# The end of the first layer's experts: where the retention weights are split, when a tile's expert sum is added, and when two modulation chunks are computed

## The chip, the cores and the metric

One core of one Trainium2 chip runs the whole kernel. The metric is the device time of one execution in microseconds (us). Five engines work side by side, each through its own instruction queue: TensorE (PE, with its weight loads as PEld), VectorE (DVE), ScalarE (ACT), GpSimd (POOL) and SyncE (SP), which here issues most of the loads. Dependencies between engines are semaphores.

## The reference, cut to what matters

The network has two layers over 256 latent tokens and 256 context tokens of width 1024, in fp32. Layer 0 is a Fourier and neighbourhood-attention mixer and a mixture of 16 experts; layer 1 is retention with four heads and another mixture. What concerns this change is the seam between them:

```
f  = moe_ffn(tok, ...)                     # tok: 256 context rows, then 256 latent rows
hc = hc + g2c * f[:n_c]                    # layer 0's end, context
h  = h  + g2  * f[n_c:]                    # layer 0's end, latent
xm = modulate(rmsnorm(h,  g), sh1, sc1)    # layer 1's beginning
cm = modulate(rmsnorm(hc, g), sh1c, sc1c)
q, k, v, g = split(xm @ w_in)              # retention, latent
_, kc, vc, _ = split(cm @ w_in)            # retention, context (keys and values are used)
```

The modulation vectors are `silu(c) @ ada_w[layer] + ada_b[layer]`, six of width 1024 for each layer.

## The kernel before, in words

**Numbers.** Every fp32 product of weight and activation is made as three fp32r matmuls: each operand is split in a high half (ScalarE rounds it, `whi`, L176) and a low half (the difference, `wlo`, L178). `weight` loads a 1 MB tile of [128, 2048] by one DMA on SP's queue (`load`, L157) and splits it in two pieces of [128, 1024]. Its `pool` argument says how many of the two low halves GpSimd computes instead of VectorE. The raw tiles lie in a ring of slots, four of them at the end of the experts; a load waits until the slot's former tile has been read by all its users. The halves lie in a second ring, six slots there.

**Tokens.** The tokens are four tiles of 128 rows in `h`: tiles 0 and 1 are latent, 2 and 3 are context. The experts run one after the other; experts 0 to 14 add their rows into a DRAM sum `F` by an indirect DMA of GpSimd. `add_sum(t)` (L798 to L802) loads tile t of that sum into one of two buffers (`facc[:, t % 2]`), multiplies it by the gate row and adds it to `h`. Expert 15 does not scatter: its output stays on the chip as `yh`, `yl` (L1085, L1086), and `combine(t)` brings it to tile t's rows by a one-hot matmul (L792, L793), a multiplication from PSUM (L782) and an addition (L783), for two halves of the width.

**The seam.** `moe0_tail` normalises the context tiles first: `norm_scale` squares a tile on ScalarE (L322), runs a chain of one-column Newton steps for the inverse root on VectorE (L199 to L210, L324, L325) and scales the tile (L327). `norm_mod` transposes it on TensorE (L338), modulates it (L343, L346) and splits it into `r_xc` (L348, L349). Then come the v projection of the first context tile (`vproj`) and the key projection of both (`k_ctx`) for head 0. `retention` goes on with the second context tile's v projection, the same norms for the latent tiles, and then the latent v projections.

**Modulation chunks.** Each chunk of 512 columns of `ada_w` is two raw tiles and 64 small matmuls (L274), whose sum stands in a PSUM buffer until its finish adds the bias (L282) and writes the row to DRAM. Chunks 4 and 5 of layer 1 are the gate `g1`, which is first used behind the retention heads. `ada_step` does the next chunk of `ada_q`.

**Order.** A planner orders each engine's instructions by when they are ready in its model, and by the order in which they are written where several are. `issue_after(i)` adds an edge: what the block writes on the engine of `i` comes after `i` on that engine; other engines' instructions in the block get no edge. On the chip each engine runs its list in order.

Of the kernel before, what the change touches and what calls it, by code (L numbers as in the profile page):

```python
# [110 lines left out]
class Net:  # L111
# [609 lines left out]
    def moe0_tail(self, ep, psp, hps):  # L721
        nc, X = self.nc, self.X
        xr = self.pool(self.ret_es, "r_ctx", 1, side="right")
        self.xc = [xr.tile([128, 8, 256], F32R, name=f"r_xc{i}") for i in range(2)]
        self.kc = [xr.tile([128, 2, 256], F32R, name=f"r_kc{i}") for i in range(2)]
        self.v0 = xr.tile([128, 512], F32, name="r_v0")
        self.ret_wv = wv = [self.weight(("ret_w_in", (), 4 * i, 4, 2048, 512), 2) for i in range(2)]
        self.ret_w0 = w0 = self.weight(self.ret_keys(0)[0], 2)
        self.ada_q = [(1, c) for c in (4, 5, 6, 7, 8, 9)]
        hp = hps, "h"  # L730
        after = lambda i: self.tc.issue_after(i.ins)
        x = X["xg"]
        xms = lambda: ep.tile([128, 4, 128], F32, tag="g", name="xm")
        mm, add = self.combine(2)
        last = self.norm_scale(2, x[0])
        with after(last):
            mm, add = self.combine(3)
        last = self.norm_scale(3, x[1])
        with after(last), after(mm):
            self.ada_step(hp, psp)  # L740
        for t in (0, 1):
            self.add_sum(t)
        for t in (2, 3):
            last = self.norm_mod(1, t, x[t - 2], xms, psp, *self.xc)
        with after(last):
            for t in (0, 1):
                self.combine(t)
        v = hps.tile([128, 512], F32, tag="h", name="v_ps")
        self.vproj(wv, self.xc, 0, v)
        nc.scalar.copy(self.v0, v)  # L750
        self.k_ctx(w0, hps.tile([128, 2, 256], F32, tag="h", name="k_ps"), slice(0, 256))
        self.ada_step(hp, psp)

    def vproj(self, ws, x, t, ps):
        tk = slice(128 * t, 128 * t + 128)
# [293 lines left out]
    def expert(self, e):  # L1049
        nc, X = self.nc, self.X  # L1050
        layer, NT, ep, psp, hs, R, T = (X[k] for k in ("layer", "NT", "ep", "psp", "hs", "R", "T"))
        gw = R["gw"][:, e:e + 1]
        self.e_hid(e, "moe_w1", 1)
        self.e_hid(e, "moe_w3", 0)
        self.e_tr(e + 1)
        self.e_gather(e + 1 + len(X["xg"]))
        self.e_hid(e, "moe_w3", 1)
        g = ep.tile([128, 512], F32, tag="g", name="g")
        nc.scalar.activation(g, hs[e, "moe_w1"], AF.Silu)
        nc.vector.tensor_tensor(g, g, hs[e, "moe_w3"], ALU.mult)  # L1060
        gh = ep.tile([128, 4, 128], F32R, tag="gh", name="gh")
        gl = ep.tile([128, 4, 128], F32R, tag="gl", name="gl")
        self.transpose_split(g, 4, gh, gl, psp)
        self.e_hid(e + 1, "moe_w1", 0)
        if e < 15:
            y = ep.tile([128, D], F32, tag="y", name="y")
        else:
            S = ep.tile([128, T], F32R, name="S", bufs=1)
            self.onehot(S, NT, R["tokf"][:, e:e + 1])
            yh = ep.tile([128, D], F32R, name="yh", bufs=1)  # L1070
            yl = ep.tile([128, D], F32R, name="yl", bufs=1)
            X["y"] = S, yh, yl
            wts = [self.weight(("moe_w2", (layer, e), 0, 4, 512 * n, 512)) for n in range(2)]
            for t in (2, 3):
                self.add_sum(t)
        for n in range(2):
            ns = slice(512 * n, 512 * n + 512)
            wt = wts[n] if e == 15 else self.weight(("moe_w2", (layer, e), 0, 4, 512 * n, 512))
            ps = X["yps"].tile([128, 512], F32, tag="y", name="y_ps")
            for k in range(4):  # L1080
                self.mm3(ps, (gh[:, k], gl[:, k]), self.wk(wt, k), k == 0, k == 3)
            if e < 15:
                nc.scalar.activation(y[:, ns], ps, AF.Copy, scale=gw)  # L1083
            else:
                nc.scalar.activation(yh[:, ns], ps, AF.Copy, scale=gw)  # L1085
                nc.vector.scalar_tensor_tensor(yl[:, ns], ps, gw, yh[:, ns].bitcast(F32), ALU.mult, ALU.subtract)  # L1086
        if e < 15:
            nc.gpsimd.indirect_dma_start(out=self.F[:, :],  # L1088
                                         out_offset=bass.IndirectOffsetOnAxis(ap=R["tok"][:, e:e + 1], axis=0),
                                         in_=y, in_offset=None, bounds_check=T - 1, oob_is_err=False,  # L1090
                                         compute_op=ALU.add)
# [556 lines left out]
```

## Time and profile before

| | us |
|---|---|
| median of 3 runs (lowest 1306.22, highest 1993.7) | 1308.19 |
| the profiled execution | 1309.31 |
| its span, from the first to the last instruction | 1307.3 |

| engine | busy us | share of the span |
|---|---|---|
| PE | 1202.9 | 92% |
| PEld | 946.0 | 72% |
| DVE | 944.2 | 72% |
| ACT | 752.0 | 58% |
| POOL | 143.2 | 11% |

The shares are averages over the whole span; the seam is about 50 us of it, so it has to be read by stretch. In the profile's tables a row names line, engine, operation, output and inputs, the shape, how often, and in brackets how long the engine had been idle before it and which instruction ended that. Operations of the same line that follow each other are merged in a timeline (x2, x3). A matmul's end is modelled, and successive matmuls overlap.

### The profile page before, as it was taken

What the parts mean: (1) busy time and instruction counts of PE and PEld (TensorE: products, weight loads), DVE (VectorE), ACT (ScalarE), POOL (GpSimd) and SP (SyncE); (2) the same over time, 40 slices, a digit from 0 to 9 for tenths busy, and PEclk for the clock granted to TensorE, in tenths of its full rate; (3) what the DMA queues carried; (4) which work ended last, traced back from release to release, by engine and by line L of the source; (5) the groups of instructions that cost most, each with busy time, mean ns of one, the idle gap of its engine ahead of it and who ended that gap; (6) DMA issues with size and microseconds to landing.
All of it is one profiled execution on the core that took longest, in us unless ns stands there. A gap on an engine that the chain in (4) does not pass through costs nothing. (4 is left out here: it accounts for less than half of the span.)

```text
span 1307.3 us, 18799 instructions
## 1 busy us (share of the span) xinstructions
PE 1202.9 (92%) x7081; PEld 946.0 (72%) x7081; DVE 944.2 (72%) x1584; ACT 752.0 (58%) x1116; POOL 143.2 (11%) x138
## 2 busy tenths in 40 slices
PE   4999999897699999999589999999996999999994
PEld 3777666475588888777368888898775778877673
DVE  4755566866698988898876554554657889888985
ACT  3754565723488887877534333343434778767672
POOL 2010001201221112110500000000003100000010
PEclk8999999999799999999889999999998999999997
DMA  9766663444899999999745345432749899889980
GB/s 357 251 243 249 239 217 124 150 146 144 328 366 383 372 361 358 359 361 363 276 162 200 133 159 202 158 114 97 284 169 380 326 342 379 329 328 352 329 325 9
DMA packets 61413, 340.60 MB, mean 261 GB/s; under 512 B 10300, under 2 KB 14908, under 8 KB 24704
## 3 DMA queue, kind: packets, MB, share of 16 engines
q1 hardware_dynamic: 47232, 307.26, 62.5%
q0 software_dynamic: 11344, 27.62, 6.7%
q10 hardware_dynamic: 2736, 4.41, 1.0%
q8 instruction: 59, 0.97, 0.3%
q14 instruction: 42, 0.34, 0.1%
HBM read 331.64 MB, written 18.40 MB: 268 GB/s over the span
## 5 line engine op out<-in xcount | busy, mean ns | idle before, releaser
L178 DVE TENSOR_TENSOR wlo<-raw,whi 128x1024 fp32r<-128x1024 f32 x465 | 551.1, 1219 | 115.6 <-ACT whi L176 113.6
L176 ACT ACTIVATE whi<-raw 128x1024 fp32r<-128x1024 f32 x476 | 480.0, 1053 | 101.1 <-PE qk_ps L314 22.1
L314 PE MATMUL h_ps<-wlo,xh 128*128 128x512 f32 x512 | 206.9, 404 | 5.5 <-DVE wlo L178 5.4
L313 PE MATMUL h_ps<-whi,xh 128*128 128x512 f32 x512 | 205.1, 401 | 1.2 <-ACT xh L669 1.2
L315 PE MATMUL h_ps<-whi,xl 128*128 128x512 f32 x512 | 204.3, 399 | 0.0
L314 PEld LDWEIGHTS h_ps<-wlo,xh 128*128 128x128 f32 x512 | 96.9, 189 | 38.6 <-DVE wlo L178 18.8
L313 PEld LDWEIGHTS h_ps<-whi,xh 128*128 128x128 f32 x512 | 97.2, 190 | 22.7 <-ACT xh L669 1.6
L315 PEld LDWEIGHTS h_ps<-whi,xl 128*128 128x128 f32 x512 | 97.0, 189 | 20.3 <-DVE xl L670 0.3
L274 PE MATMUL ada_ps<-raw,cT 128*32 128x128 f32 x1536 | 54.5, 280 | 1.1 <-DMA raw<-in_ada_w 1.1
L313 PE MATMUL y<-whi,gh 128*128 128x512 f32 x128 | 51.6, 403 | 0.7 <-ACT gh L669 0.7
L313 PE MATMUL y_ps<-whi,gh 128*128 128x512 f32 x128 | 51.2, 400 | 0.7 <-ACT gh L669 0.7
L315 PE MATMUL y<-whi,gl 128*128 128x512 f32 x128 | 50.8, 405 | 0.8 <-DVE gl L670 0.6
L314 PE MATMUL y<-wlo,gh 128*128 128x512 f32 x128 | 51.1, 399 | 0.3 <-DVE wlo L178 0.3
L314 PE MATMUL y_ps<-wlo,gh 128*128 128x512 f32 x128 | 51.1, 399 | 0.0
L274 PEld LDWEIGHTS ada_ps<-raw,cT 128*32 128x32 f32 x1536 | 42.1, 111 | 12.1 <-issue 8.6
L315 PE MATMUL y_ps<-whi,gl 128*128 128x512 f32 x128 | 50.3, 403 | 0.1
L1088 POOL DMA_INDIRECT moe_sum<-y,tok x15 | 27.9, 1857 | 153.8 <-ACT y L1083 153.8
L669 ACT ACTIVATE gh<-tsp 128x512 fp32r<-128x512 f32 x32 | 19.1, 596 | 43.4 <-PE tsp L666 43.2
L313 PE MATMUL qk_ps<-xhi,whi 128*128 128x512 f32 x96 | 39.4, 411 | 0.0
L314 PE MATMUL qk_ps<-xlo,whi 128*128 128x512 f32 x96 | 38.8, 404 | 0.0
L315 PE MATMUL qk_ps<-xhi,wlo 128*128 128x512 f32 x96 | 38.4, 400 | 0.0
L1541 POOL DMA_INDIRECT out_dram<-hg,tok x4 | 6.6, 1662 | 274.5 <-DVE hg L1535 219.5
(438 smaller groups left out, 2423.9 us busy)
## 6 DMA issues: line engine op xcount, KB each, us to landing
raw<-in_moe_w SPq DMA_DIRECT2D x192, 1024.0 KB, 7.9
raw<-in_ada_w SPq DMA_DIRECT2D x48, 1024.0 KB, 5.1
raw<-in_ret_w_in SPq DMA_DIRECT2D x24, 1024.0 KB, 4.9
raw<-in_mixab_w_in SPq DMA_DIRECT2D x10, 1024.0 KB, 6.8
raw<-in_ret_w_out SPq DMA_DIRECT2D x8, 1024.0 KB, 4.8
raw<-in_mixab_w_out SPq DMA_DIRECT2D x4, 1024.0 KB, 6.7
bias<-in_rpb ACTq DMA_DIRECT2D x12, 256.0 KB, 4.9
g<-mod POOLq DMA_DIRECT2D x6, 512.0 KB, 4.7
```

The source lines that it names most:

```text
L176: self.nc.scalar.activation(hi, r, AF.Copy)
L178: eng.tensor_tensor(lo, r, hi.bitcast(F32), ALU.subtract)
L274: mm = nc.tensor.matmul(ps[32 * j:32 * j + 32, 0:128], self.cT[:, kk, :], raw[:, k, 128 * j:128 * j + 128], start=(kk == 0), stop=(kk == 7 ...
L313: mm(out, lh, rh, start=first, stop=False)
L314: mm(out, lh, rl, start=False, stop=False)
L315: self.mm_last = mm(out, ll, rh, start=False, stop=last)
L669: nc.scalar.activation(hi[:, b0:b0 + w], tv, AF.Copy)
L1088: nc.gpsimd.indirect_dma_start(out=self.F[:, :], out_offset=bass.IndirectOffsetOnAxis(ap=R["tok"][:, e:e + 1], axis=0), in_=y, in_offset=N ...
L1541: self.nc.gpsimd.indirect_dma_start(out=self.out[:, :], out_offset=bass.IndirectOffsetOnAxis(ap=idx, axis=0), in_=x, in_offset=None, bound ...
```

## The change

The six low halves of the three retention weight tiles (two for v, one for the keys) were GpSimd's; they become VectorE's. The two tiles for v are written behind tile 3's scale, so their low halves follow it on VectorE; the tile for the keys is written behind the last of the modulated context rows. Tile 3's expert sum is added in the tail behind tile 2's norm and no longer within expert 15. Tile 3's combine loses its edge. Chunks 4 and 5 are loaded and multiplied ahead of tile 3's norm, with both finishes behind the modulated context rows; before, chunk 4 came after the second norm and chunk 5 at the end. The sums of tiles 0 and 1 move behind the modulated context rows too.

```diff
-        self.ret_wv = wv = [self.weight(("ret_w_in", (), 4 * i, 4, 2048, 512), 2) for i in range(2)]
-        self.ret_w0 = w0 = self.weight(self.ret_keys(0)[0], 2)
-        self.ada_q = [(1, c) for c in (4, 5, 6, 7, 8, 9)]
+        self.ada_q = [(1, c) for c in (6, 7, 8, 9)]
...
         mm, add = self.combine(2)
         last = self.norm_scale(2, x[0])
+        self.add_sum(3)
+        mm, add = self.combine(3)
+        fin = [self.ada_mm(1, c, hp, psp) for c in (4, 5)]
+        last = self.norm_scale(3, x[1])
         with after(last):
-            mm, add = self.combine(3)
-        last = self.norm_scale(3, x[1])
-        with after(last), after(mm):
-            self.ada_step(hp, psp)
-        for t in (0, 1):
-            self.add_sum(t)
+            self.ret_wv = wv = [self.weight(("ret_w_in", (), 4 * i, 4, 2048, 512)) for i in range(2)]
         for t in (2, 3):
             last = self.norm_mod(1, t, x[t - 2], xms, psp, *self.xc)
         with after(last):
+            self.ret_w0 = w0 = self.weight(self.ret_keys(0)[0])
+            for f in fin:
+                f()
             for t in (0, 1):
+                self.add_sum(t)
                 self.combine(t)
...
         self.k_ctx(w0, hps.tile([128, 2, 256], F32, tag="h", name="k_ps"), slice(0, 256))
-        self.ada_step(hp, psp)
...
             wts = [self.weight(("moe_w2", (layer, e), 0, 4, 512 * n, 512)) for n in range(2)]
-            for t in (2, 3):
-                self.add_sum(t)
+            self.add_sum(2)
```

## Rows read from the trace of the kernel before

**Rows 1.** Stretches: length, busy PE PEld DVE ACT POOL, granted clock, DMA share, GB/s.
```profile
637.80:642.60 4.80, 2.64 (x9) 1.16 (x7) 3.82 (x6) 4.11 (x5) 4.02 (x2) 0.96 1.00 423
642.60:655.20 12.60, 0.12 (x1) 0.00 (x0) 11.50 (x15) 3.34 (x6) 10.80 (x5) 0.50 0.82 291
655.20:668.00 12.80, 7.96 (x81) 5.28 (x82) 11.27 (x27) 3.99 (x10) 0.26 (x1) 0.77 0.63 239
668.00:693.30 25.30, 25.15 (x249) 21.64 (x248) 16.22 (x48) 10.27 (x25) 1.59 (x3) 0.97 0.42 142
693.30:960.00 266.70, 265.66 (x1645) 228.15 (x1642) 145.65 (x229) 103.39 (x141) 6.44 (x12) 1.00 0.46 169
```

**Rows 2.** VectorE's timeline, 641 to 656 us: start, duration, instruction, [idle before].
```profile
641.06 1.29 DVE L782 TENSOR_TENSOR gtmp<-f_ps,g 128x512 f32<-128x512 f32 x2 [0.27 <-PE f_ps L793]
642.26 4.32 DVE L783 TENSOR_TENSOR h<-h,gtmp 128x512 f32<-128x512 f32 x2
647.38 1.44 DVE L324 TENSOR_TENSOR rms_ss<-nss 128x1 f32<-128x1 f32 x1 [0.79 <-ACT xg L322]
...
649.42 1.70 DVE L206 SCALAR_TENSOR_TENSOR rs_a<-rs_y,rs_h 128x1 f32<-128x1 f32 x1
651.15 2.26 DVE L210 SCALAR_TENSOR_TENSOR rs_y<-rs_a,rs_y 128x1 f32<-128x1 f32 x1
...
654.34 0.75 DVE L327 TENSOR_SCALAR xg<-h,rs_y 128x1024 f32<-128x1024 f32 x1
```

**Rows 3.** GpSimd's timeline, 638 to 656 us.
```profile
638.58 14.82 POOL L178 TENSOR_TENSOR wlo<-raw,whi 128x1024 fp32r<-128x1024 f32 x6 [15.22 <-ACT whi L176]
```

**Rows 4.** VectorE's timeline, 660 to 683 us.
```profile
660.02 1.22 DVE L801 TENSOR_TENSOR facc<-facc,g 128x1024 f32<-128x1024 f32 x1
...
666.48 0.75 DVE L327 TENSOR_SCALAR xg<-h,rs_y 128x1024 f32<-128x1024 f32 x1
...
676.23 1.28 DVE L783 TENSOR_TENSOR h<-h,gtmp 128x512 f32<-128x512 f32 x2
677.60 0.16 DVE L324 TENSOR_TENSOR rms_ss<-nss 128x1 f32<-128x1 f32 x1
...
678.36 0.22 DVE L206 SCALAR_TENSOR_TENSOR rs_a<-rs_y,rs_h 128x1 f32<-128x1 f32 x1
...
679.52 0.15 DVE L210 SCALAR_TENSOR_TENSOR rs_y<-rs_a,rs_y 128x1 f32<-128x1 f32 x1
682.12 0.69 DVE L768 SCALAR_TENSOR_TENSOR r_kc<-k_ps,r_kc 128x512 fp32r<-128x512 f32 x1 [2.45 <-ACT r_kc L767]
```

**Rows 5.** The low halves' line over the whole span: ns min/median/max.
```profile
L178 DVE TENSOR_TENSOR wlo<-raw,whi x465: 1192/1218/1277, 24.8 to 1286.3; 128x1024 fp32r<-128x1024 f32 x155
```

**Rows 6.** ScalarE's timeline, 637 to 641 us.
```profile
637.43 2.00 ACT L176 ACTIVATE whi<-raw 128x1024 fp32r<-128x1024 f32 x2 [1.05 <-DMA raw<-in_ret_w_in]
639.34 0.67 ACT L1085 ACTIVATE yh<-y_ps,gw 128x512 fp32r<-128x512 f32 x1
```

**Rows 7.** SP's queue (issue of loads), and raw tiles' landing times, 618 to 690 us.
```profile
629.44 2.17 SPq L157 DMA_DIRECT2D raw<-in_ret_w_in  x3
...
DMA to landing us min/median/max: 4.8/5.9/11.0
```

**Rows 8.** TensorE's timeline, 637 to 694 us.
```profile
637.59 0.39 PE L315 MATMUL y_ps<-whi,gl 128*128 128x512 f32 x1
655.62 1.94 PE L274 MATMUL ada_ps<-raw,cT 128*32 128x128 f32 x32
...
681.38 2.37 PE L274 MATMUL ada_ps<-raw,cT 128*32 128x128 f32 x74
...
683.88 0.48 PE L313 MATMUL v_ps<-whi,r_xc 128*128 128x512 f32 x1
...
689.56 0.82 PE L338 MATMUL nT<-cst,og 128*128 128x128 f32 x6
...
693.34 0.50 PE L313 MATMUL v_ps<-whi,r_xl 128*128 128x512 f32 x1
```

## The prediction

> **What bounds the kernel now.** I read the busy times by stretch first, then the VectorE, GpSimd, ScalarE, DMA-queue and TensorE timelines of one place: the end of layer 0's experts, 637 to 694 us.
>
> TensorE sets the pace after this place: from 693.3 to 960 us it is busy for 265.66 of 266.70 us at full granted clock [rows 1]. Before that it is not: it idles 12.5 of the 12.6 us from 642.6, and 4.8 of the next 12.8 [rows 1]. With 2.2 us just ahead (2.64 busy of 4.80) and 0.15 behind, that is 19.6 us of idle time, the most that this change can win. What is won here arrives at the end only because of that dense stretch: its 1% of idle time leaves nowhere for an earlier start to be absorbed. VectorE is nearly full in the same stretches (11.50 of 12.60, 11.27 of 12.80) but has 9.1 us free in the 25.3 us after them [rows 1].
>
> Why TensorE waits: the first transposes need tile 2's normalised rows, which VectorE finishes at 655.09, the last row of [rows 2]. Its chain there is slow. GpSimd runs six low halves of retention weights from 638.58 to 653.40 [rows 3]. Inside that span a pair of adds took 4.32 us, the one-column sum 1.44, the two Newton steps 1.70 and 2.26 [rows 2]; the same instructions later took 1.28, 0.16, 0.22 and 0.15 [rows 4]. The excess is 3.04 + 1.28 + 1.48 + 2.11 = 7.9 us. A product from PSUM, 1.29 us a pair, was not slowed [rows 2]. Nor is DMA traffic the cause: an SBUF-SBUF product at 660.02 took its usual 1.22 us [rows 4] while 239 GB/s moved [rows 1].
>
> The Trainium skill, "SBUF — State Buffer", section "Who interferes with whom", says that a VectorE instruction with two SBUF inputs and a GpSimd instruction that reads SBUF exclude each other for a whole instruction. By it the full 7.9 us go once GpSimd has no such work; were it wrong and the slow rows due to something else, this term would be 0 and the forecast would land where the second rival does. The unslowed PSUM product agrees with it.
>
> **Part by part.** Clock times are those of the trace.
>
> *GpSimd's six low halves go to VectorE.* Removed from the first chain: 7.9 us. Added: 6 x 1.22 = 7.3 us of VectorE [rows 5], but behind the second normalisation. GpSimd's later work is only small row writes, which nobody in this stretch waits for.
>
> *ScalarE.* The second half of yh ran at 639.34, behind two high halves that began at 637.43 [rows 6]. That half of y was ready when its matmuls ended, at 638.0 [rows 8]. With the ada loads taking the first slots, those high halves are not there yet: -1.3 us. Bound: 0, if the planner puts other splits there.
>
> *Tile 3's sum and combine.* Its two full-width instructions (2 x 1.2 = 2.4 us) ran before the second yl. They may now fall in the wait for y's second half (about 636.4 to 638.7, as long as they are): 0, or 2.4 us if that cover is gone and they enter the chain. The combine's VectorE half (four instructions, 2 x 1.28 = 2.5 us) is no longer held behind tile 2's scale, so it can enter tile 2's chain while ScalarE squares: +2.5 at worst, 0 at best; I take 2.4, since the old order kept tile 3's adds out by an explicit edge.
> Tile 2 is then ready at 655.1 - 1.3 - 7.9 + 2.4 = 648.3.
>
> *Tile 3's normalisation.* It ended at 667.23 because its one-column steps alternated with the sums of tiles 0 and 1, one of which is the 1.22 us row at 660.02 [rows 4]. These move behind the modulation. Alone, the chain is 2.1 us (677.60 to 679.67) plus 0.75 for the scale [rows 2, 4]: ready at 648.3 + 2.8 = 651.1, 16 us sooner.
>
> *Weights.* Four ada loads (1 MB each) now stand on SP's queue ahead of the three retention loads, with two small bias loads. The first load that was issued at 629.44 [rows 7] served a ScalarE split at 637.43 that had waited for it [rows 6]: 8.0 us. The ada halves take that place, are read by 32 matmuls each (1.94 us at the low clock), and free slots from about 639.5 and 641. With 8.0 us more the value weights land at 647.5 and 649, and with a high half of 1.05 us each (2.00 a pair [rows 6]) their last low half can begin at 651. VectorE is at 651.1 then: hidden, with about 3 us to spare behind the first halves. Landings in this stretch run from 4.8 to 11.0 us [rows 7]; 11.0 uses that spare up.
> VectorE then does four low halves (4.9) and tile 2's two lower halves of modulated rows (the key product's, of the same shape, took 0.69 [rows 4]): 657.3.
>
> *TensorE.* The v projection, 24 matmuls, takes 5.7 us (683.88 to 689.56 for the second one [rows 8]); it can start at about 656 and end by 662.7. Tile 3's modulation (two such halves, 1.4, and four pieces of 128x128, which hold the elements of one 0.69 us instruction: 0.7 to twice that, I take 1.3) and the key weights' two low halves (2.4) end at 662.4; the key projection, 48 matmuls of half the width, takes the same 5.7 us, which put its end at 681.38 [rows 8]: now 668.4. The second ada chunk, 64 of the 74 matmuls in 2.37 us (2.05 us), stood here [rows 8] and is now in the idle gap; so the next v projection, 5.7 us, ends at 674.1. The transposes and the filler chunk that took 3.8 us (689.56 to 693.34 [rows 8]) bring the latent v projection to 677.9, against 693.34: -15.4.
>
> *VectorE's floor for the same point.* From 662.4: two ada finishes (128x128 each; at most 0.69, I take 0.3 each), sums of tiles 0 and 1 (4 x 1.22), their combine (8 x 0.64, the pairs of 1.28 and 1.29): 673.0. The normalisation of tile 1 adds squares (two halves on ScalarE, like yh's 0.67 [rows 6]: 1.4), chain and scale (2.8): 677.2. Transposing, modulating and splitting took the same 3.8 us: 681.0, which is -12.3. The key product's lower half, which held the line until 682.12 with tile 0's scale behind it [rows 4], stands earlier now.
>
> **The sum.** VectorE's floor is the later one; the first latent projection needs only tile 0's rows, so I take a little more, -12.5 us: 1309.3 of the profiled execution becomes 1296.8. That execution lies 1.1 us above the median of the runs, 1308.19, so the forecast is 1296. A second count bears it out: up to 693.3 VectorE has 11.7 us of idle time [rows 1]; with 7.9 out, 7.3 in and 1.3 from ScalarE it could come forward by 13.6 us if it never waited.
> The clock is the loosest term. It was granted at 0.50 in the empty stretch and 0.77 after it [rows 1], that is wholly and then about half the time at 1.2 of 2.4 GHz. With ada matmuls in the gap it may rise earlier (a gain of about 2 us), or the v projection may run wholly at the low level (5.7 us more on TensorE, of which 3.1 hide below VectorE's floor).
>
> **Rivals.**
> *The weights come late and VectorE's queue stands behind them (slower).* VectorE works in order: at 682.12 it sat 2.45 us for the key product while tile 0's scale, whose chain had ended at 679.67, ran only after it [rows 4]. All that stands behind the value weights' low halves, from the last of them to the latent v projection, is 25 us in my count (656 to 681). So the change wins if the last low half ends before 668.3 and loses after. It would end later if the planner left the ada matmuls where they were, beginning at 655.62 behind the first transpose [rows 8]: slots free at 657.5 and 660, loads land after up to 11.0 us at 671, high and low half 2.3: 673.5, that is +5: 1313. For it: both ada chunks now hold all four slots. Against it: in the written order these matmuls stand ahead of the transposes, and TensorE has 12.5 us with nothing else.
> The Trainium skill, "TensorE: Matmul & The Clock Gate", specification table at its head, lists VectorE's queue as strict first-in first-out, which is the rule this rival rests on; the 2.45 us agree.
> *VectorE binds (little gain).* As much goes on VectorE as comes off (7.3 against 7.9 us). If its other waits stay as long as they are, only 0.6 + 1.3 + 2.05 (the ada chunk off TensorE's path) remain, about 4 us, or less: 1304. For it: 11.50 of 12.60 busy. Against it: those waits are mostly for TensorE, 9.1 us after 668 [rows 1], and TensorE comes earlier.
> *All idle time of TensorE goes.* Up to 19.6 us: 1289. Against it: tile 2's chain cannot end before about 646, and the ada chunks fill only part of what is left.
>
> **Chances.** Forecast (8 to 17 us won, 1291 to 1300) 0.62; VectorE binds (0 to 8 won, 1300 to 1308) 0.20; late weights (slower, 1308 to 1318) 0.12; nearly all idle time won (1288 to 1291) 0.06. The range 1289 to 1308 leaves out the slower case and a little below. A measurement tells about 2% from no change, 26 us here; the idle time to be won is less than that, and the slower case costs 5 us. So faster by over 2% has 0.02, slower 0.02, within 2% 0.96.
>
> **What would show it.** Right: no GpSimd low half after 638, the pair of adds back near 1.3 us and the one-column steps near 0.2; tile 2's scale near 648 and tile 3's near 651; ada matmuls between 638 and 648; value weights landed before tile 3's scale; the latent v projection near 681. Wrong: VectorE's low halves waiting for loads, one-column steps between full-width ones in tile 2's chain, or a latent v projection that waits for VectorE as long as before.

## The result, and the profile after

| | before, us | changed, us | ratio, 95% interval |
|---|---|---|---|
| first timing, 5 runs each | 1306.22 | 1299.76 | 0.9949 [0.9934, 0.9963] |
| again, beside the experiments | 1308.00 | 1300.43 | 0.9939 [0.9921, 0.9957] |
| once more | 1307.69 | 1299.28 | 0.9939 [0.9921, 0.9957] |

The change wins 6.5 to 8.4 us by the medians, where 12 were forecast. One of the first five runs of the kernel before took 1993.7 us and enters no ratio. The spans of the two profiled executions, 1307.3 and 1298.8, differ by 8.5.

Since the stretch ahead of the seam varies from run to run by some 3 us, I count from a mark, T: the start of expert 15's last matmul into `y_ps`, the first row of [rows 8], at 637.59 before and 639.20 after.

The stretches of [rows 1] in the changed kernel (length, busy PE PEld DVE ACT POOL, granted clock, DMA share, GB/s; the last ends at 952 us):

```profile
637.80:642.60 4.80, 4.80 (x56) 3.31 (x54) 4.40 (x6) 0.88 (x2) 0.00 (x0) 1.00 1.02 420
642.60:655.20 12.60, 7.76 (x105) 5.68 (x105) 10.84 (x37) 6.01 (x14) 0.00 (x0) 0.76 0.97 370
655.20:668.00 12.80, 11.80 (x53) 9.71 (x54) 12.10 (x19) 8.18 (x14) 1.81 (x3) 0.84 0.83 297
668.00:693.30 25.30, 22.85 (x168) 18.93 (x167) 19.05 (x51) 11.10 (x25) 0.55 (x1) 0.93 0.42 157
693.30:952.00 258.70, 257.66 (x1609) 221.94 (x1608) 141.60 (x219) 99.57 (x134) 6.22 (x11) 1.00 0.46 168
```

TensorE's idle time up to 693.3 has shrunk from 19.6 us to 8.3 (0 + 4.84 + 1.00 + 2.45), by 11.3. GpSimd has nothing in the first two stretches, and the dense stretch behind is as dense as before.

VectorE's timeline of the changed kernel, beside [rows 2]:

```profile
643.58 1.28 DVE L783 TENSOR_TENSOR h<-h,gtmp 128x512 f32<-128x512 f32 x2
644.78 1.28 DVE L782 TENSOR_TENSOR gtmp<-f_ps,g 128x512 f32<-128x512 f32 x2
645.98 0.15 DVE L324 TENSOR_TENSOR rms_ss<-nss 128x1 f32<-128x1 f32 x1
646.05 0.68 DVE L783 TENSOR_TENSOR h<-h,gtmp 128x512 f32<-128x512 f32 x1
...
647.68 0.22 DVE L206 SCALAR_TENSOR_TENSOR rs_a<-rs_y,rs_h 128x1 f32<-128x1 f32 x1
647.94 0.16 DVE L210 SCALAR_TENSOR_TENSOR rs_y<-rs_a,rs_y 128x1 f32<-128x1 f32 x1
...
649.03 0.75 DVE L327 TENSOR_SCALAR xg<-h,rs_y 128x1024 f32<-128x1024 f32 x1
...
651.77 0.75 DVE L327 TENSOR_SCALAR xg<-h,rs_y 128x1024 f32<-128x1024 f32 x1
...
654.04 2.36 DVE L178 TENSOR_TENSOR wlo<-raw,whi 128x1024 fp32r<-128x1024 f32 x2 [0.89 <-ACT whi L176]
```

The pair of adds is back from 4.32 to 1.28 us, the one-column sum from 1.44 to 0.15, the Newton steps from 1.70 and 2.26 to 0.22 and 0.16. Tile 3's combine (644.78, 646.05) now runs inside tile 2's chain.

### The profile page after: what moved, and what is told of

It is laid out like the page before. It is cut to its first block, busy times and chain, and to the rows that moved or that the text cites. A ratio compares the mean times of both kernels' runs of the same rounds, so it can differ in the third digit from the quotient of the medians.

```text
span 1298.8 us, 18788 instructions
## 1 busy us (share of the span) xinstructions
PE 1202.1 (93%) x7081; PEld 945.2 (73%) x7081; DVE 942.4 (73%) x1590; ACT 752.4 (58%) x1116; POOL 130.3 (10%) x132
## 5 line engine op out<-in xcount | busy, mean ns | idle before, releaser
L178 DVE TENSOR_TENSOR wlo<-raw,whi 128x1024 fp32r<-128x1024 f32 x471 | 558.5, 1220 | 116.4 <-ACT whi L176 114.3
L669 ACT ACTIVATE gh<-tsp 128x512 fp32r<-128x512 f32 x32 | 19.1, 597 | 43.6 <-PE tsp L666 43.4
L1540 POOL DMA_INDIRECT out_dram<-hg,tok x4 | 9.9, 2476 | 272.3 <-DVE hg L1534 220.5
```

The source lines that it names most:

```text
L178: eng.tensor_tensor(lo, r, hi.bitcast(F32), ALU.subtract)
L669: nc.scalar.activation(hi[:, b0:b0 + w], tv, AF.Copy)
L1540: self.nc.gpsimd.indirect_dma_start(out=self.out[:, :], out_offset=bass.IndirectOffsetOnAxis(ap=idx, axis=0), in_=x, in_offset=None, bound ...
```

## The experiments

Each run below is told by its median, its ratio to the kernel before (runs of the same chip, beside it) and three marks of its trace, from T: the end of tile 2's scale, the end of tile 3's, and the start of the latent v projection. The kernel before and the changed one have been traced more than once; the marks here are the first trace's. The changed kernel's time is the one taken on the chip of the other rows.

| kernel | median us | ratio | tile 2 | tile 3 | latent v |
|---|---|---|---|---|---|
| before | 1308.06 | 1 | 17.50 | 29.64 | 55.75 |
| changed | 1300.43 | 0.9939 [0.9921, 0.9957] | 10.58 | 13.32 | 44.80 |
| GpSimd only writes | 1300.24 | 0.9931 [0.9909, 0.9952] | 8.55 | 20.69 | 47.06 |
| VectorE, old place | 1303.73 | 0.9963 [0.9951, 0.9975] | 19.32 | 26.89 | 52.25 |
| changed, GpSimd back | 1299.70 | 0.9930 [0.9910, 0.9950] | 10.59 | 13.33 | 48.03 |
| changed, chunks back | 1298.30 | 0.9920 [0.9898, 0.9941] | 9.79 | 12.76 | 45.49 |

**1. GpSimd only writes.** The kernel before, where GpSimd fills the low halves of head 0's context v and key weights with zeros instead of computing them, so it reads nothing. Head 0 lacks those low halves.

```diff
-            eng.tensor_tensor(lo, r, hi.bitcast(F32), ALU.subtract)
+            eng.tensor_tensor(lo, r, hi.bitcast(F32), ALU.subtract) if pool < 3 else eng.memset(lo.bitcast(F32), 0.0)
...
-        self.ret_wv = wv = [self.weight(..., 2) for i in range(2)]
-        self.ret_w0 = w0 = self.weight(self.ret_keys(0)[0], 2)
+        self.ret_wv = wv = [self.weight(..., 3) for i in range(2)]
+        self.ret_w0 = w0 = self.weight(self.ret_keys(0)[0], 3)
```

> The kernel before with one thing changed: the six low halves of the tail's retention weights are not computed; GpSimd fills them with zeros instead (a write that reads nothing), so head 0's context values and keys come out without their low halves. VectorE's instructions and their order are those of before. Theory (the GpSimd subtractions, which read SBUF, held back VectorE's two-input instructions): the pair of adds back to about 1.3 us, Newton steps to about 0.2, tile 2's scale done 9.6 us after the start of expert 15's last y matmul instead of 17.5, and 5 to 7 us won overall: ratio 0.9945 to 0.996. Rival (any GpSimd work of this size, or the DMA traffic, slows VectorE): the slow rows stay, 16 to 17.5 us, ratio 0.999 to 1.001.

Its VectorE timeline holds the instructions of [rows 2] in the same order:

```profile
642.13 1.28 DVE L783 TENSOR_TENSOR h<-h,gtmp 128x512 f32<-128x512 f32 x2
644.21 0.16 DVE L324 TENSOR_TENSOR rms_ss<-nss 128x1 f32<-128x1 f32 x1 [0.80 <-ACT xg L322]
...
644.97 0.22 DVE L206 SCALAR_TENSOR_TENSOR rs_a<-rs_y,rs_h 128x1 f32<-128x1 f32 x1
...
646.32 0.75 DVE L327 TENSOR_SCALAR xg<-h,rs_y 128x1024 f32<-128x1024 f32 x1
```

Every duration is the fast one, and tile 2 is ready 8.95 us sooner. The chain's first product started 1.12 us sooner (640.87, T + 2.35, against 641.06, T + 3.47); the other 7.83 are the excess that the prediction added up as 7.9. The time falls by 7.8 us, more than the 5 to 7 expected, and by the medians as much as with the whole change. That instructions lasting 0.15 to 0.22 us took 1.4 to 2.3 beside GpSimd's subtractions was the cost, not VectorE's amount of work.

The six writes take 0.95 us each, and the last four of them, in three rows, show that all are over by 639.70, before this chain begins:

```profile
635.02 0.95 POOL L178 MEMSET wlo<- 128x1024 f32 x1 [3.89 <-PE y_ps L314]
636.41 1.89 POOL L178 MEMSET wlo<- 128x1024 f32 x2 [0.44 <-PE y_ps L314]
638.75 0.95 POOL L178 MEMSET wlo<- 128x1024 f32 x1 [0.45 <-PE y_ps L314]
```

So the chain shows what the stalls cost, and not by itself that a write does no harm. That is shown by VectorE's sums with two SBUF inputs, which ran beside the writes:

```profile
634.99 2.35 DVE L801 TENSOR_TENSOR facc<-facc,g 128x1024 f32<-128x1024 f32 x2
637.26 2.35 DVE L802 TENSOR_TENSOR h<-h,facc 128x1024 f32<-128x1024 f32 x2
```

In the kernel before the same two pairs took 2.35 us as well, with GpSimd idle. The DMA engines are no cause of the slow rows either. From 642.1 to 646.4 us, with the chain fast, they are 0.99 busy at 414 GB/s; in the kernel before, with the chain slow, 0.82 at 291 [rows 1].

**2. VectorE, old place.** The kernel before, the six low halves on VectorE and nothing moved.

```diff
-        self.ret_wv = wv = [self.weight(..., 2) for i in range(2)]
-        self.ret_w0 = w0 = self.weight(self.ret_keys(0)[0], 2)
+        self.ret_wv = wv = [self.weight(...) for i in range(2)]
+        self.ret_w0 = w0 = self.weight(self.ret_keys(0)[0])
```

> The kernel before with the six low halves on VectorE and nothing moved. The written order then puts all six ahead of tile 2's combine on VectorE. Theory (what counts is what stands in the norm chain of tile 2): no stall from GpSimd, but the chain waits for the weights to land and then for 7.3 us of low halves, so tile 2's scale ends 21 to 24 us after the start of expert 15's last y matmul (before: 17.5), and the kernel is 3 to 8 us slower than before: ratio 1.002 to 1.006. Rival (taking the work off GpSimd is the whole gain, wherever VectorE does it): 5 to 7 us faster, ratio 0.9945 to 0.996.

```profile
640.71 6.89 DVE L178 TENSOR_TENSOR wlo<-raw,whi 128x1024 fp32r<-128x1024 f32 x6
647.51 1.28 DVE L782 TENSOR_TENSOR gtmp<-f_ps,g 128x512 f32<-128x512 f32 x2
...
651.45 1.23 DVE L801 TENSOR_TENSOR facc<-facc,g 128x1024 f32<-128x1024 f32 x1
...
656.96 0.75 DVE L327 TENSOR_SCALAR xg<-h,rs_y 128x1024 f32<-128x1024 f32 x1
...
664.53 0.75 DVE L327 TENSOR_SCALAR xg<-h,rs_y 128x1024 f32<-128x1024 f32 x1
```

The halves do stand ahead of tile 2's chain, and tile 2 is 1.8 us later than before. Yet the kernel is faster than before, not slower as I expected, though by less than the rival said (0.9945 to 0.996). I had counted only tile 2. With tile 2 late, the planner's sums of tiles 0 and 1 (the row at 651.45 and three like it) fell into tile 2's chain instead of tile 3's; tile 3 came 2.75 us sooner, and the latent projection 3.5. For tile 2 the halves start the chain's first product 5.65 us later (T + 9.12 against T + 3.47), which is less than the 7.9 us of the stalls, and the sums add about 4; tile 3 is spared them. A first effect was sized without the next stop.

**3. Changed, GpSimd back.** The changed kernel, with the six low halves on GpSimd again, behind tile 3's scale.

```diff
-            self.ret_wv = wv = [self.weight(...) for i in range(2)]
+            self.ret_wv = wv = [self.weight(..., 2) for i in range(2)]
...
-            self.ret_w0 = w0 = self.weight(self.ret_keys(0)[0])
+            self.ret_w0 = w0 = self.weight(self.ret_keys(0)[0], 2)
```

> The changed kernel with the six low halves back on GpSimd, all else as changed. They can only run once the later loads have landed, about 15 us after expert 15's last y matmul, and take 14.4 us on GpSimd, beside tile 3's split, the latent sums and combines. Theory (the tail is a chain; GpSimd is slower at it and holds back two-input instructions): the v and key projections wait for the low halves, and the latent v projection starts 2 to 5 us later than in the changed kernel (44.8 us after the last y matmul's start there): ratio to before 0.996 to 1.000. Rival (VectorE's amount of work is the bound): 7.3 us less on VectorE, 3 to 6 us faster than the changed kernel: ratio 0.989 to 0.993.

Its GpSimd, then its VectorE:

```profile
651.29 16.84 POOL L178 TENSOR_TENSOR wlo<-raw,whi 128x1024 fp32r<-128x1024 f32 x6 [29.14 <-ACT whi L176]
```

```profile
654.63 2.36 DVE L349 TENSOR_TENSOR r_xc<-xm,r_xc 128x512 fp32r<-128x512 f32 x1
...
662.92 2.99 DVE L801 TENSOR_TENSOR facc<-facc,g 128x1024 f32<-128x1024 f32 x1
...
666.44 2.78 DVE L802 TENSOR_TENSOR h<-h,facc 128x1024 f32<-128x1024 f32 x1
...
670.94 1.21 DVE L801 TENSOR_TENSOR facc<-facc,g 128x1024 f32<-128x1024 f32 x1
```

The two-input instructions beside GpSimd are slow again (2.99 against 1.21 for the same sum once GpSimd has stopped), and the latent projection is 3.2 us later than in the changed kernel, inside the 2 to 5 expected. Transfers do not explain it: at the slow sum of 2.78 us the DMA engines are 0.15 busy at 23 GB/s. Tiles 2 and 3 are as early, because the work stands behind them. In the time those 3.2 us don't show: 0.9930, no worse than the changed kernel, where 0.996 to 1.000 was expected. Moving the work behind the norms is what pays; which engine does it there is not told apart by the medians.

**4. Changed, chunks back.** The changed kernel with chunks 4 and 5 where they were.

```diff
-        self.ada_q = [(1, c) for c in (6, 7, 8, 9)]
+        self.ada_q = [(1, c) for c in (4, 5, 6, 7, 8, 9)]
-        fin = [self.ada_mm(1, c, hp, psp) for c in (4, 5)]
         last = self.norm_scale(3, x[1])
+        with after(last), after(mm):
+            self.ada_step(hp, psp)
...
-            for f in fin:
-                f()
...
+        self.ada_step(hp, psp)
```

> The changed kernel with modulation chunks 4 and 5 back where they were (4 behind the second norm, 5 at the end). Theory (moving them fills idle time of TensorE and takes 2 us off its path, but VectorE's chain sets the latent norm, so most of this is hidden): 1 to 3 us slower than the changed kernel, with the retention weights landing some 7 us sooner: ratio to before 0.996 to 0.9975. Rival (the move is where the gain comes from): ratio 0.9985 to 1.001. Rival (its cost, the late weights, eats its gain): as fast as the changed kernel or faster, 0.993 to 0.9955.

The seam is 0.7 us longer by the latent projection, and the time is not longer at all: 0.9920, where the theory said 0.996 to 0.9975. A single second run took 1299.44 us, beside 1299.28 for the changed kernel. The chunks' move has no gain that the runs can show.

**5. The kernel before, again.** The same code a second time, as a measure of chance.

> The kernel before once more, for a second profile: how far its marks move from one execution to the next. Expected: up to 2 us in when expert 15 ends (637.6 in the first), under 0.5 us in the stretch from there to the latent v projection (55.75), about 1 us in what follows it (614.0); ratio 0.998 to 1.002.

1307.87 us, ratio 0.9997 [0.9986, 1.0008]; its marks repeat to 0.06 us (17.48, 29.62, 55.70). Up to the latent projection, marks counted from T are therefore sharp, while T itself moved by 0.9.

**6. The changed kernel, again.**

> The changed kernel once more, on one chip with the runs below. If the trace's 10 us at the end of the tail are real and the first 6.7 us were a chance draw of what lies ahead of it: ratio 0.9915 to 0.9935. If some of the gain is really given back outside the tail: 0.994 to 0.996.

> The changed kernel once more. In its two traces so far layer 1's experts give back 2.7 and 3.7 us of the tail's gain between experts 4 and 5, where TensorE waits for its weights; in e4_ada_back, with the same instruction order there, 0.4. Theory 'timing alone' (the weights arrive just in time there, and which run waits is chance): the give-back differs from trace to trace, anywhere from 0 to 4 us, and this run's ratio is 0.992 to 0.996. Rival 'the change costs it' (two modulation chunks gone from retention shift something in the weights' stream every time): again 2.5 to 4 us.

The marks of the two (10.58, 12.98, 44.48; 10.59, 13.20, 44.58) repeat the first trace's to 0.01 us for tile 2, to 0.3 for tile 3 and the projection. The ratio, 0.9939 both times, lies between the two ranges expected of the first repeat and inside the second's. What came after the seam differs, and is told with number 9.

**7. Tile 0's norm ahead.** In the changed kernel tile 0's squares and Newton steps stand in retention, where they alternate with tile 1's. Here they are written behind tile 0's combine.

```diff
                 self.add_sum(t)
                 self.combine(t)
+                if t == 0:
+                    self.r0 = self.norm_stat(0, x[0])
...
-                for t in range(2):
-                    self.norm_scale(t, x[t])
+                nc.vector.tensor_scalar(x[0], h[:, 0], self.r0, None, ALU.mult)
+                self.norm_scale(1, x[1])
```

> The changed kernel, with tile 0's squares and Newton chain written in the tail, behind its own combine and ahead of tile 1's sum; only its scale stays in the retention. Theory (VectorE's order at the latent norms is what was left over: tile 0's chain stood behind tile 1's sums, and the two chains then alternated): tile 0's scale ends at 37 us after the last y matmul's start instead of 40.1, tile 1's at 41 instead of 43.3, the latent v projection starts at 42 to 43 instead of 44.8 and at full clock, and the kernel is 2 to 3 us faster than the changed one on this chip. Rival (TensorE's own work bounds that point): within 1 us of the changed kernel.

1299.23 us, 0.9935 [0.9921, 0.9949], latent projection at 45.25: nothing won, where 42 to 43 was forecast. Tile 1's scale did come sooner, at T + 41.99 against 43.34, but its transposes then waited 1.60 us, until 680.33, for ScalarE's modulation of tile 0.

**8. And the sums joined.** As 7, and for tiles 0 and 1 the part from `F` and the part of expert 15 are added before the one product with `g2`, instead of a product and an add for each.

```diff
+            V.tensor_tensor(f[:, ns], ps, f[:, ns], ALU.add)
+        V.tensor_tensor(f, f, self.g2[t // 2], ALU.mult)
+        V.tensor_tensor(h[:, t], h[:, t], f, ALU.add)
```

> As the last, and the sums of tiles 0 and 1 joined with their combine: the product is added to the loaded sum first, and one gate multiplication and one addition serve both, 3.5 us of VectorE a tile instead of 4.7. Theory (VectorE's amount of work sets the end of the tail): 2 x 1.2 us sooner again, tile 1's scale at 38.5 to 39.5, the latent v projection at 41 to 42.5, 3 to 5 us faster than the changed kernel. Rival (TensorE's own work, 24 + 48 + 24 matmuls and the filler chunk, ends at about 40.5 and bounds it): no better than the last one by more than 0.7 us.

> The changed kernel with tile 0's squares ahead and the sums of tiles 0 and 1 in one with the combine, once more beside the changed kernel. Theory (VectorE's order in the tail is what is left): 1 to 4 us under the changed kernel, ratio 0.990 to 0.994. Rival (TensorE's own length sets the tail by now): as the changed kernel within 1 us, 0.993 to 0.995.

1296.71 us, 0.9921 [0.9905, 0.9937], then 1297.99, 0.9932 [0.9914, 0.9949]; latent projection at 43.85 and 43.61, where 41 to 42.5 was forecast. It is 3.7 and 1.3 us below the changed kernel of the same chip, and the intervals overlap both times.

**9. Given back behind the seam.** How far a kernel is ahead of the kernel before (both from their T, first trace of that) does not stay the same behind the seam. In the table, retention is the dense stretch of the prediction (ScalarE's rows from 90 us behind T on); "before the wait" is the last `h_ps` matmul ahead of TensorE's transposes of `g` (L666) at about 1057 us, in layer 1's fourth expert; "last expert" is ScalarE's `g` in layer 1's last expert.

| kernel | latent projection | retention | before the wait | last expert | span's end |
|---|---|---|---|---|---|
| changed, first trace | -10.95 | -9.9 | -11.5 | -10.1 | -10.1 |
| changed, second | -11.27 | -11.0 | -11.5 | -9.0 | -7.7 |
| changed, third | -11.17 | -9.6 | -10.6 | -9.4 | -8.2 |
| number 4, first | -10.26 | -9.9 | -9.7 | -10.6 | -10.6 |
| number 4, second | -10.23 | -9.9 | -10.4 | -10.8 | -10.9 |
| number 10 | -12.80 | -10.0 | -11.1 | -11.5 | -11.5 |
| number 3 | -7.72 | -7.5 | -7.8 | -8.9 | -9.0 |
| number 1 | -8.69 | -8.7 | -9.5 | -10.6 | -9.3 |

The first and the third trace of the changed kernel lose 1.0 and 1.5 us in the latent projection itself, at a low clock behind an idle gap; the second kept the full clock there and lost 0.2. From before the wait to the last expert the changed kernel gives back 1.4, 2.5 and 1.2 us, and no other row of the table gives back any. (The recorded expectations put more on this place, 2.7 and 3.7 and 0.4 for number 4; they go by ScalarE's `g` of experts that they call 4 and 5, one of which starts 1.3 us later against TensorE in the kernel before than in the others, so each of these figures is 1.3 too large. They count the experts from 1.) In that measure the third trace gave back 2.4: within the 0 to 4 of chance, just under the rival's 2.5 to 4. Number 7 gives back 0.7 at the wait, number 8 0.7 and 2.9 in its two traces.

Between retention and the wait the shifts move as well. Where layer 1's experts begin, TensorE mostly waits for weights: in the changed kernel it is busy for 1.66 of the 10 us from 994.3, with the DMA engines 1.01 busy at 416 GB/s, in the kernel before for 3.37 of the 10 us from 1002.6, at 1.01 and 419.

> The changed kernel with chunks 4 and 5 in their old place, once more. Theory 'timing alone': the give-back between layer 1's experts 4 and 5 is not 0.4 us again for certain, but anything from 0 to 4. Rival 'the change costs it': again under 0.6 us, since the chunks stand where they were.

TensorE in that place, in the three traces of the changed kernel, then number 4's second trace:

```profile
1059.32 0.66 PE L666 MATMUL tsp<-cst,g 128*128 128x128 f32 x4 [2.36 <-DVE g L1493]
```

```profile
1057.50 0.66 PE L666 MATMUL tsp<-cst,g 128*128 128x128 f32 x4 [1.91 <-DVE g L1493]
```

```profile
1056.89 0.66 PE L666 MATMUL tsp<-cst,g 128*128 128x128 f32 x4 [2.10 <-DVE g L1493]
```

```profile
1058.11 0.66 PE L666 MATMUL tsp<-cst,g 128*128 128x128 f32 x4 [0.55 <-DVE g L1493]
```

The kernel before waits 0.9 and 1.0 there; number 4's first trace 0.1, numbers 7 and 8 waited 1.6 and 1.6 and 2.4, number 10 waits 0.6, and numbers 1 and 3 nothing. That the kernel before waits too fits that the rows below the changed kernel's gain 0.4 to 1.1 us there. Ahead of it the expert weights stream. The changed kernel's first trace, as a stretch:

```profile
1015.00:1057.00 42.00, 41.96 (x190) 33.66 (x188) 36.00 (x35) 31.87 (x36) 0.00 (x0) 1.00 0.97 359
```

TensorE is full and the DMA engines are 0.97 busy at 359 GB/s. In the second trace the wait also cost clock:

```profile
1055.00:1060.00 5.00, 3.10 (x14) 2.20 (x13) 5.00 (x6) 3.38 (x5) 0.00 (x0) 0.88 0.85 305
1060.00:1065.00 5.00, 5.00 (x19) 3.98 (x18) 2.22 (x3) 1.75 (x3) 0.00 (x0) 0.78 0.96 351
```

Columns as in the stretches above: a granted clock of 0.88 and 0.78, part of the time at 1.2 of 2.4 GHz, where the first trace kept 1.00. It gave back 2.5 us instead of 1.4. The second and third trace then lost another 1.3 and 1.2 us in the last expert, with nothing loading. The clock there was granted at 0.72 in the second, from 1275 to 1280 us, and at 0.71 in the third, from 1273 to 1278; in the first trace it was 1.00.

Chance alone is a poor reading: all six traces with moved chunks and low halves on VectorE wait 1.6 to 2.4, all three with the chunks back 0.1 to 0.6. But number 3 has moved chunks and no wait, with a seam that won less. Behind the seam, TensorE, VectorE, ScalarE and the load queue run the same order of instructions in the changed kernel and in numbers 3 and 4. The transposes wait for VectorE's `g`, which stands behind low halves of weights, and these wait for ScalarE's high halves. Where they were late, ScalarE had been idle; the changed kernel's first trace and number 4's first, whose T are 639.20 and 639.21:

```profile
1054.01 4.85 ACT L176 ACTIVATE whi<-raw 128x1024 fp32r<-128x1024 f32 x5 [2.77 <-PE h_ps L315]
```

```profile
1052.35 2.96 ACT L176 ACTIVATE whi<-raw 128x1024 fp32r<-128x1024 f32 x3 [0.33 <-issue]
```

That an earlier kernel meets loads that are paced by DMA fits this, but is not shown; which load it is, and why the chunks' place matters, stays open.

**10. Joined sums and chunks back.** Numbers 4 and 8 in one kernel.

> Both together: the fused sums, and chunks 4 and 5 where they were. Theory (the two are independent; the moved chunks add 64 matmuls and two transfers to the tail and spare as many later): within 1.5 us of the fused sums alone, 0.990 to 0.994. Rival 'the chunks' move costs the give-back in layer 1': 2 to 3 us below the fused sums alone, 0.989 to 0.991, and its trace shows under 0.6 us given back between experts 4 and 5.

1295.84 us, 0.9909 [0.9889, 0.9929]: the fastest of all, 11.9 us below the kernel before and 3.4 below the changed one, whose interval it still touches. It is 2.2 below number 8 alone, where the rival said 2 to 3 and the theory up to 1.5; its give-back, 0.9 by the measure of the expectations, is above the rival's 0.6, but of that 1.3 is the kernel before's own, and by the table it gave back nothing. Its stretch that answers to 668.0 to 693.3 us (28.8 to 54.1 from T), and its latent projection:

```profile
666.20:691.50 25.30, 25.30 (x195) 21.57 (x194) 18.48 (x47) 13.12 (x28) 0.56 (x1) 1.00 0.34 122
```

```profile
679.90 0.71 PE L340 MATMUL nT<-cst,og 128*128 128x128 f32 x5
680.37 0.48 PE L313 MATMUL v_ps<-whi,r_xl 128*128 128x512 f32 x1
```

TensorE never idles there and keeps the full clock; the latent projection starts at T + 42.95 with only part of tile 1's transposes ahead of it. In part it is early because one filler chunk (64 matmuls, 1.96 us in the changed kernel), which runs ahead of it in the other traces, runs behind it here, and in retention the kernel is ahead by 10.0 us, like number 4 with 9.9. Here VectorE is no longer the floor.

## Why the prediction was right, and where it was off

The direction, the mechanism and the range held; the gain is a half to two thirds of the forecast one. By its steps, each time from T:

| step | forecast | measured |
|---|---|---|
| tile 2's scale ends | 10.7 | 10.58 |
| tile 3's scale ends | 13.5 | 13.32 |
| first low half of the value weights starts | 13.5 | 14.84 |
| key projection starts | 25.1 | 25.96 |
| sums of tiles 0 and 1 end | 35.4 | 35.96 |
| tile 1's scale ends | 39.6 | 43.3 |
| second v projection ends | 36.5 | 40.5 |
| latent v projection starts | 43.4 | 44.80 |

**Tile 2's chain: right term by term.** The excess of 7.9 us went, as experiment 1 shows by itself. ScalarE's second half of y started at 639.63, T + 0.43, against T + 1.75 [rows 6]: the 1.3 us were there. Tile 3's combine entered the chain, as I chose: the forecast 6.8 us net measured 6.92. One thing I left at 0 or 2.4 cost some 0.6: a full-width add of tile 3's sum, 1.21 us at 639.73, stood before the second `yl`, which began at 640.86 instead of about 640.3, when ScalarE's half was done.

The Trainium skill, "SBUF — State Buffer", section "Who interferes with whom", says that a VectorE instruction with two SBUF inputs contends with a GpSimd instruction that reads SBUF, and not with one that only writes. The traces agree with both halves: 4.32 to 1.28 us with the reads gone and 1.21 to 2.99 with them back (experiments 1 and 3), and 2.35 us for a pair of sums with the writes beside them and without (experiment 1).

**The weights: right, behind ScalarE's own work.** The value loads were issued from 642.34, behind the ada loads, and ScalarE's high halves began at 652.95, right behind three modulations of its own; VectorE sat 0.89 us for the first, in the row at 654.04. ScalarE did not idle between its modulations and that high half, so the 0.89 us are its order and not shown to be late weights; the late-weights rival has a price of 0.9 at most, not 5.

**The tail: right sum, two wrong terms.** VectorE's floor was forecast at 43.4 for the latent projection, and it came at 44.80. But tile 1's normalisation ended 3.7 us later than its term:

```profile
673.88 1.28 DVE L783 TENSOR_TENSOR h<-h,gtmp 128x512 f32<-128x512 f32 x2
...
677.21 0.15 DVE L324 TENSOR_TENSOR rms_ss<-nss 128x1 f32<-128x1 f32 x1
...
677.92 0.68 DVE L1244 TENSOR_TENSOR vl<-r_v,vh 128x512 fp32r<-128x512 f32 x1
678.52 0.75 DVE L327 TENSOR_SCALAR og<-h,rs_y 128x1024 f32<-128x1024 f32 x1
...
681.79 0.75 DVE L327 TENSOR_SCALAR og<-h,rs_y 128x1024 f32<-128x1024 f32 x1
```

I gave it 1.4 + 2.8 us, as if it ran alone. Its chain alternates with tile 0's scale, tile 0's steps and two lower halves of v. What made up for most of it is that I then had the projection wait for 3.8 us of transposes and splits behind tile 1, when it needs tile 0's rows alone. TensorE, in the changed kernel:

```profile
671.54 1.96 PE L274 MATMUL ada_ps<-raw,cT 128*32 128x128 f32 x64
674.01 0.50 PE L313 MATMUL v_ps<-whi,r_xc 128*128 128x512 f32 x1 [0.51 <-DVE gtmp L782]
...
682.68 1.67 PE L338 MATMUL nT<-cst,og 128*128 128x128 f32 x8 [1.94 <-DVE og L327]
684.00 0.78 PE L313 MATMUL v_ps<-whi,r_xl 128*128 128x512 f32 x1
684.57 0.63 PE L314 MATMUL v_ps<-wlo,r_xl 128*128 128x512 f32 x1
685.00 0.63 PE L315 MATMUL v_ps<-whi,r_xl 128*128 128x512 f32 x1
```

Another filler chunk took the place of the moved one ahead of the second v projection (1.96 us at 671.54), so the 2.05 us that I took off TensorE's path there came back. TensorE then idled 1.94 us, since tile 1's transposes stood in its queue ahead of the latent projection, and the first six matmuls of that ran at the low clock: 0.43 us apart, where later ones are 0.235. That is 6 x 0.2 = 1.2 us, in a term I had called the loosest. The second trace kept the full clock there and still started the projection at T + 44.48.

**Carried to the end: the step that failed.** I forecast -12.5 at the latent projection and let all of it arrive at the end, since the dense stretch of retention (693 to 960 us) "leaves nowhere for an earlier start to be absorbed". From T, the projection came 10.95, 11.27 and 11.17 us sooner in the three traces: the two wrong terms above, which made up for each other in part. Of that, 9.9, 11.0 and 9.6 were there in retention, since the projection itself ran at the low clock in the first and third trace, and 10.1, 7.7 and 8.2 at the end. The prediction stopped at retention, as if what follows had to move along. In layer 1's experts the changed kernel waits behind a stretch of nearly full transfers and gives back 1.2 to 2.5 us, and in two of three traces the last expert loses about 1.3 more at a low clock (experiment 9). Why the wait comes in this kernel and not in number 4 stays open. In the first trace T itself lay 1.6 later than before; the other traces put it at 637.83 and 636.15, and the kernel before at 637.59 and 636.71, so as far as five traces tell it varies from run to run.

**Two slips in the arithmetic, neither of which carries the forecast.** The 11.7 us of VectorE's idle time in the second count are those from 642.6 on; with the first stretch of [rows 1] they are 12.7. And a v projection of 5.7 us that starts at 656 ends at 661.7, not 662.7; the key weights' halves at 662.4 would then set the key projection, 0.3 sooner. VectorE's floor, which gave the forecast, does not use it.

**Rivals.** "VectorE binds" had it half right: VectorE is full in the seam (12.10 of 12.80) and its tail sets the latent projection, but its waits did shrink, and the gain lies at the 8 us where that rival ended. "All idle time goes" was out of reach by 8.3 us. That the chunks' move matters, 2.05 us on TensorE's path, fell (experiment 4); the forecast itself went by VectorE's floor, which does not have that term.

## What to carry to other kernels

Look for one-column instructions that take microseconds: they show that something shuts an engine out, and what to move is the other engine's work, behind the chain that is waited for, before asking which engine should do it. A gain at one place is carried by a dense stretch only as far as that stretch goes; read every later stretch in which transfers are near full, and every idle gap behind which the clock is low, as a place that can take some of it back. When work leaves a queue, list what the planner puts into the hole: here a filler chunk and the other tiles' sums came in, once as a cost and once as a gain.

## What the runs showed of the hardware

The spread of one kernel's runs goes in part with the clock. The six runs of number 10 took 1292.4 and 1292.5 us at a mean granted clock of 0.974, 1294.7 and 1297.0 at 0.973, and 1297.4 and 1298.8 at 0.971; of the changed kernel's third timing 1296.7 at 0.975 and 1301.6 at 0.971. But three runs of the kernel before on the same chip took 1303.17, 1307.69 and 1309.35, all at 0.971. A spread of 5 to 6 us is most of what the change wins, which is why differences of 2 or 3 us between variants stay inside the intervals here while marks in a trace repeat to 0.3.

A GpSimd subtraction of 128x1024 was itself slower beside VectorE's two-input work: 2.81 us each in experiment 3 (16.84 by 6), 2.47 each in [rows 3], and VectorE did the same in 1.22 [rows 5]. Elsewhere in the kernel before it took GpSimd 2.34 to 2.50.
